# The second product of the MLP by Strassen's scheme, one product of quarters behind the other in four PSUM banks each

## The chip, the core and the metric

The kernel runs on one core of a Trainium2 chip. Five engines work side by side and meet only at semaphores: TensorE (PE in the profile, with its weight loads as PEld), VectorE (DVE), ScalarE (ACT), GpSimd (POOL) and SyncE (SP). Each takes its instructions in order. Operands lie in SBUF, 128 partitions wide; matmul results go to PSUM, which has eight banks of 128 x 512 floats. DMA transfers are issued here by SP. The metric is the device time of one execution in microseconds, as the median of several.

## The reference

One layer of a decoder over 1024 tokens of width 1024: a mixer with two kinds of attention, and an MLP. The change is in the last part of the MLP:

```python
h = rms_norm(x, pre_ffn_g[l])
u = causal_depthwise_conv(h @ w_up[l], conv_w[l], conv_b[l])
gate, val = jnp.split(u, 2, axis=-1)
y = (jax.nn.gelu(gate, approximate=True) * val) @ w_down[l]
x = x + rms_norm(y, post_ffn_g[l])
```

With G for `gelu(gate) * val` (1024 tokens x 2816 features), the last product is Y = G W with W = `w_down` (2816 x 1024). After it come the sum of squares of each row of Y, the gain `post_ffn_g`, and the addition of x.

## The kernel before

Every product is made of float32 operands that are split in two: `hi`, rounded by a copy on ScalarE (line 140), and `lo`, the rest, by a subtraction on VectorE (line 137). A product is then three matmuls, hi x hi, lo x hi and hi x lo, into the same bank. A tile of 128 x 512 thus costs one load of 256 KB, one ACTIVATE and one TENSOR_TENSOR before TensorE can use it. `load_raw` loads such a tile into a pool of five buffers, `slot_w` gives the pair of buffers for hi and lo.

The first product of the MLP (h @ w_up) runs over 22 blocks of 128 features. From block 3 on, `seven` computes a block by seven products of quarters: halves of tokens, of the inner dimension and of gate and value. `weights` makes the sums and splits of the weight quarters one block ahead. `gated` does the convolution and the gate for a block and stores G, transposed, to DRAM as `c_d[f]` (line 1073); this is the last thing done for a block.

The second product, from line 1209 on, runs over halves of the tokens (`half`). For each of 22 feature blocks `down_operands` loads and splits the 512 tokens of `c_d[f]` (tiles `gh`, `gl`) and the two halves of `w_down[f]` (tiles `whi`, `wlo`, from pool `wpool` or `dw`). `product(f, m)` multiplies 128 tokens of it by both halves of the outputs, six matmuls, into two banks that belong to m: four m and two banks each take all eight banks for the whole half. For the last four blocks (`LAST`) the program goes m by m, so that the rows of one m are complete before those of the next. A complete m is finished by lines 1240 to 1249: squares and their sum on ScalarE, the gain on VectorE, the reciprocal root by ten small operations on VectorE (`rsqrt`, lines 153 to 168), then one operation for each half of the outputs that scales and adds x (`x2`), and a store of it.

The operands of feature blocks 0 and 1 are loaded and split during the last block of the first product (line 1201), into the pool `early` and into free slots of `wpool`. Pools open and close like a stack from two sides of SBUF, left and right; a tile of a new pool waits for the tiles that had its place. When the first product ends, its pools close (`mix` with the activations, `uf`, `xw`, `early`, `cv` on the right, `wb` and `mid` on the left), and `gp2` on the left and `dw` on the right take their place.

The order of the instructions on each engine, SP's queue too, is made by a planner: it goes by the order of the program, by when it expects things to be ready, and lets what stands in `tc.high_priority` go ahead. The order of the trace is therefore not always that of the program.

Of the kernel before, what the change touches and what calls it, by code (L numbers as in the profile page):

```python
# [24 lines left out]
P = 128  # L25
S = 1024
D = 1024
# [6 lines left out]
NF = FF // P  # L34
# [7 lines left out]
NEG = -1.0e30  # L42

FULL = 3
LAST = 4
MIX_UNITS = {3: (0,), 4: (1,), 5: (2, 4), 6: (3, 5), 7: (6, 7)}
START_GATES, A_FILLS, B_GATES = 2, ("pggg", "pvgg", "wpgg", "PVg"), 3
SLOTS = 18
# [37 lines left out]
def trunk(ctx: ExitStack, tc: tile.TileContext, a, out):  # L86
    nc = tc.nc
    dma = nc.sync.dma_start

    def open_pool(stack, name, bufs=1, side="left", **kw):  # L90
        if "space" not in kw:
            kw.update(side=side, reuse_waits="tile")
        return stack.enter_context(tc.tile_pool(name=name, bufs=bufs, **kw))
# [17 lines left out]
    def slot_w(pool=None):  # L111

        return [(pool or wpool).tile([P, 512], F32R, tag=t, name=n, bufs=6) for t, n in (("wh", "whi"), ("wl", "wlo"))]

    def load_raw(src, pool=None):
        raw = (pool or raws_in[-1]).tile([P, 512], F32, tag="raw", name="raw", bufs=3 if pool else None)
        dma(raw, src)
        return raw

# [19 lines left out]
    def split(hi, lo, src, eng=None):  # L139
        nc.scalar.activation(hi, src, AF.Copy)  # L140
        sub(eng or nc.vector, lo, src, hi)
# [29 lines left out]
    def halves():  # L171
        return [slice(i * 512, (i + 1) * 512) for i in range(2)]
# [142 lines left out]
    with ExitStack() as st0:  # L315
# [54 lines left out]
        for n, i in enumerate(FIRST_GATES):  # L370
            t = prep.tile([P, S], F32, tag=f"raw{n}", name="gate")
# [16 lines left out]
        for half, sl in enumerate(halves()):  # L388
            row = psum(F32, pt, "pt")
# [314 lines left out]
    for n in range(2):  # L704
        t = mask_2.rearrange("p (k r) -> p r k", r=2)[:, n]
# [237 lines left out]
    def any_psum():  # L943
        return next(psums)()

    with st2:
# [48 lines left out]
        for m in range(8):  # L995
# [5 lines left out]
            pss = []  # L1001
# [128 lines left out]
    def weights(f):  # L1130

        a11, a12, a21, a22 = (load_raw(a["w_up"][2 * f + part][:, sl]) for part in range(2) for sl in halves())
        ws = {}

        def put(name, src):
            ws[name] = slot_w(wb if len(ws) % 2 else None)
            split(*ws[name], src)

        def combined(name, x, y, op):
            t = mid.tile([P, 512], F32, tag="s", name=name, bufs=4)  # L1140
            nc.vector.tensor_tensor(t, x, y, op=op)
# [41 lines left out]
        plus(c12, "p3", c12)  # L1183
        return us

    def down_operands(half, f, pool, bufs, w_pool):

        raw = load_raw(c_d[f][:, halves()[half]], pool if w_pool else None)
        g = [pool.tile([P, 512], F32R, tag=t, name=t, bufs=bufs) for t in ("gh", "gl")]
        split(*g, raw)  # L1190
        us = []
        for sl in halves():
            us.append(slot_w(w_pool))
            split(*us[-1], load_raw(a["w_down"][f][:, sl]))
        return g, us
# [10 lines left out]
    st_x.close()  # L1206


    gp2 = open_pool(ctx, "gp2")
    dw = open_pool(ctx, "dw", side="right")  # L1210
    gpost2 = gp2.tile([P, D], F32, name="gpost2")
    dma(gpost2, a["post_ffn_g"].partition_broadcast(P))
    for half in range(2):
        pss = [psum(F32, pt, "pt") for _ in range(2)] + [any_psum() for _ in range(6)]

        def product(f, m):
            (gh, gl), us = have[f]
            tk = slice(m * P, (m + 1) * P)
            for ps, (wh, wl) in zip(pss[2 * m : 2 * m + 2], us):
                nc.tensor.matmul(ps, gh[:, tk], wh, start=f == 0, stop=False)  # L1220
                nc.tensor.matmul(ps, gl[:, tk], wh, start=False, stop=False)  # L1221
                nc.tensor.matmul(ps, gh[:, tk], wl, start=False, stop=f == NF - 1)  # L1222

        for f in range(NF):
            if half or f not in have:

                with tc.high_priority(offset=60 if half == 0 and f < 4 else 0):
                    have[f] = down_operands(half, f, gp2, 6, dw)
            if f < NF - LAST:
                for m in range(4):  # L1230
                    product(f, m)
        for m in range(4):
            rows = slice((4 * half + m) * P, (4 * half + m + 1) * P)
            x2 = gp2.tile([P, D], F32, tag="x2", name="x2", bufs=3)
            dma(x2, x2_d[rows, :])
            sq, yg = (gp2.tile([P, D], F32, tag=n, name=n, bufs=2) for n in ("sq", "yg"))
            s2 = tiny.tile([P, 2], F32, tag="sm", name="s2")
            for f in range(NF - LAST, NF):
                product(f, m)
            for n, w in enumerate(halves()):  # L1240
                ps = pss[2 * m + n]
                nc.scalar.activation(sq[:, w], ps, AF.Square, accum_out=s2[:, n : n + 1])
                nc.vector.tensor_tensor(yg[:, w], ps, gpost2[:, w], op=ALU.mult)  # L1243
            ss = tiny.tile([P, 1], F32, tag="ss1", name="ss1")
            nc.vector.tensor_tensor(ss, s2[:, 0:1], s2[:, 1:2], op=ALU.add)
            r = rsqrt(ss, D, tiny, "r1")
            for w in halves():
                nc.vector.scalar_tensor_tensor(x2[:, w], yg[:, w], r, x2[:, w], op0=ALU.mult, op1=ALU.add)
                dma(out[rows, w], x2[:, w])


def units(w, rows, cols):
# [51 lines left out]
```

## Time and profile before

| | us |
|---|---|
| median of 3 runs (1812.74 to 1817.44) | 1813.17 |
| the profiled execution's own time | 1812.37 |
| its span, first to last instruction | 1810.6 |
| PE busy in the span | 1756.2 |
| DVE busy in the span | 1251.5 |
| ACT busy in the span | 846.8 |
| second product, first matmul to PE's end | 1546.4 to 1794.0 |
| from there to the end of the span | 16.6 |

The page of the profile gives the busy time of each engine, the same in forty slices of the span, and the chain of work that ended last. A matmul record overlaps the next, so that a busy PE isn't PE at its peak; the pace of matmuls is read from their starts. A row of a group shows its line, engine and operation, the tiles written and read, the count, busy time and mean, and the idle time before it with what ended it. SPq stands for SP's queue of transfers: the time of a record there is that from its issue on, with waits between those that a record merges.

### The profile page before, as it was taken

How to read it: one execution, taken by the hardware profiler on the slowest of the kernel's cores; microseconds unless marked ns; L12 is line 12 of the kernel's file. 1: busy time of each engine (PE TensorE's matmuls, PEld its weight loads, DVE VectorE, ACT ScalarE, POOL GpSimd, SP SyncE). 2: the span in 40 equal slices, each digit the busy share in tenths (PEclk: the TensorE clock that was granted, in tenths of full speed). 3: DMA queues.
4: the chain of work that ended last, by engine and by line, in shares of the span. 5: the costliest groups of instructions: out<-in, count | busy, mean ns of one | idle time of the engine just before them, and what ended most of it. 6: DMA issues, size and time to landing. Idle time of an engine off the chain costs nothing.

```text
span 1810.6 us, 24293 instructions
## 1 busy us (share of the span) xinstructions
PE 1756.2 (97%) x8886; PEld 1488.2 (82%) x8886; DVE 1251.5 (69%) x2509; ACT 846.8 (47%) x1555; POOL 51.0 (3%) x78
## 2 busy tenths in 40 slices
PE   9998999999999999999999999999999999999996
PEld 7987788788888888888777788878888888788785
DVE  4677787775555666555767677999999998434634
ACT  6375455544555644555554332554444343334331
POOL 0000000000000000000001301200000000000000
PEclk9999999999999999999999999999999999999998
DMA  8511121212131334222575421122222222644741
GB/s 268 165 52 37 59 71 59 82 41 65 51 97 53 100 118 146 67 92 94 166 249 195 156 100 64 47 101 98 89 81 76 94 81 88 200 143 142 235 135 64
DMA packets 99831, 195.52 MB, mean 108 GB/s; under 512 B 16304, under 2 KB 23152, under 8 KB 99712
## 3 DMA queue, kind: packets, MB, share of 16 engines
q1 hardware_dynamic: 91616, 182.97, 30.5%
q10 hardware_dynamic: 8096, 11.01, 1.7%
q8 instruction: 69, 1.13, 0.3%
q14 instruction: 50, 0.41, 0.1%
HBM read 150.27 MB, written 43.66 MB: 107 GB/s over the span
## 4 chain that ended last, share of the span: by engine, by line
PE 77%; DVE 9%; DMA 7%; ACT 3%; issue 3%; SPq 0%; POOL 0%; DVEq 0%; ACTq 0%
PE acc L145 14%; PE acc L144 14%; PE acc L146 14%; PE acc L435 3%; PE acc L437 3%; PE acc L436 3%; PE acc L1220 3%; PE acc L1221 3%; PE acc L1222 3%; PE acc L987 2%; PE acc L988 2%; PE acc L986 2%; DMA gl<-gt_d 1%; PE o L481 1%; PE pt L469 1%
## 5 line engine op out<-in xcount | busy, mean ns | idle before, releaser
L140 ACT ACTIVATE whi<-raw 128x512 fp32r<-128x512 f32 (+1 forms) x316 | 195.1, 626 | 342.5 <-PE acc L146 138.0
L137 DVE TENSOR_TENSOR wlo<-raw,whi 128x512 fp32r<-128x512 f32 (+1 forms) x313 | 225.5, 728 | 173.8 <-ACT whi L140 155.5
L144 PE MATMUL acc<-xh,whi 128*128 128x512 f32 x744 | 297.1, 401 | 4.8 <-DVE t L418 2.9
L145 PE MATMUL acc<-xh,wlo 128*128 128x512 f32 x744 | 297.8, 400 | 1.4 <-DVE wlo L137 1.4
L146 PE MATMUL acc<-xl,whi 128*128 128x512 f32 x744 | 295.4, 399 | 0.0
L144 PEld LDWEIGHTS acc<-xh,whi 128*128 128x128 f32 x744 | 140.9, 190 | 33.9 <-DVE t L418 3.3
L145 PEld LDWEIGHTS acc<-xh,wlo 128*128 128x128 f32 x744 | 141.3, 190 | 29.6 <-DVE wlo L137 1.6
L146 PEld LDWEIGHTS acc<-xl,whi 128*128 128x128 f32 x744 | 141.7, 190 | 28.9
L144 PE MATMUL acc<-mh,whi 128*128 128x512 f32 x400 | 156.3, 391 | 1.8 <-ACT whi L140 1.6
L145 PE MATMUL acc<-mh,wlo 128*128 128x512 f32 x400 | 156.3, 391 | 0.2 <-DVE wlo L137 0.2
L146 PE MATMUL acc<-ml,whi 128*128 128x512 f32 x400 | 156.1, 391 | 0.0
L435 PE MATMUL acc<-whi,xh 128*128 128x256 f32 x512 | 147.4, 288 | 0.0
L437 PE MATMUL acc<-wlo,xh 128*128 128x256 f32 x512 | 146.8, 287 | 0.0
L436 PE MATMUL acc<-whi,xl 128*128 128x256 f32 x512 | 146.7, 287 | 0.0
L417 ACT ACTIVATE t<-acc 64x512 f32<-64x512 f32 (+1 forms) x160 | 94.6, 591 | 44.8 <-PE acc L146 42.3
L1172 DVE TENSOR_TENSOR u<-acc,u 128x512 f32<-128x512 f32 x133 | 90.4, 683 | 26.6 <-PE acc L146 26.5
L1220 PE MATMUL acc<-whi,gh 128*128 128x512 f32 x264 | 103.3, 395 | 1.4 <-DVE yg L1243 1.4
L1221 PE MATMUL acc<-whi,gl 128*128 128x512 f32 x264 | 102.7, 389 | 0.0
L1222 PE MATMUL acc<-wlo,gh 128*128 128x512 f32 x264 | 101.6, 389 | 0.0
L436 PEld LDWEIGHTS acc<-whi,xl 128*128 128x128 f32 x512 | 97.7, 191 | 0.8
L435 PEld LDWEIGHTS acc<-whi,xh 128*128 128x128 f32 x512 | 97.8, 191 | 0.6
L437 PEld LDWEIGHTS acc<-wlo,xh 128*128 128x128 f32 x512 | 97.7, 191 | 0.5
(287 smaller groups left out, 3694.9 us busy)
## 6 DMA issues: line engine op xcount, KB each, us to landing
raw<-in_w_in SPq DMA_DIRECT2D x126, 256.0 KB, 2.8
raw<-in_w_up SPq DMA_DIRECT2D x88, 256.0 KB, 2.8
raw<-in_w_down SPq DMA_DIRECT2D x88, 256.0 KB, 3.3
c_d<-c SPq DMA_DIRECT2D x22, 512.0 KB, 2.7
raw<-c_d SPq DMA_DIRECT2D x44, 256.0 KB, 3.5
gl<-gt_d SPq DMA_DIRECT2D x16, 512.0 KB, 5.7
gt_d<-gate ACTq DMA_DIRECT2D x26, 256.0 KB, 2.0
og_d<-osb SPq DMA_DIRECT2D x12, 512.0 KB, 4.5
```

Of the source, the lines that this page charges most:

```text
L137: eng.tensor_tensor(lo, src, hi.bitcast(F32), op=ALU.subtract)
L140: nc.scalar.activation(hi, src, AF.Copy)
L144: nc.tensor.matmul(o, sh, mh, start=first, stop=False)
L145: nc.tensor.matmul(o, sl, mh, start=False, stop=False)
L146: nc.tensor.matmul(o, sh, ml, start=False, stop=last)
L417: nc.scalar.activation(t1[dst], ps[src], AF.Copy)
L435: nc.tensor.matmul(ps, xh[:, k, tk], wh[:, w], start=k == 0, stop=False)
L436: nc.tensor.matmul(ps, xl[:, k, tk], wh[:, w], start=False, stop=False)
L437: nc.tensor.matmul(ps, xh[:, k, tk], wl[:, w], start=False, stop=k == KC - 1)
L1220: nc.tensor.matmul(ps, gh[:, tk], wh, start=f == 0, stop=False)
L1221: nc.tensor.matmul(ps, gl[:, tk], wh, start=False, stop=False)
L1222: nc.tensor.matmul(ps, gh[:, tk], wl, start=False, stop=f == NF - 1)
```

## The change

Y is cut in quarters: tokens in two halves i, features in two halves j of 11 blocks (`NH`), outputs in two halves k. With A for the quarters of G and B for those of W, the seven products are, in the order in which they run:

| | left | right | added to |
|---|---|---|---|
| p1 | A11 | B11 | c11, u |
| p5 | A21 + A22 = S1 | B12 - B11 = T1 | c22, c12 |
| p6 | S1 - A11 = S2 | B22 - T1 = T2 | u |
| p7 | A11 - A21 | B22 - B12 | c21, c22 |
| p3 | A12 - S2 | B22 | c12 |
| p2 | A12 | B21 | c11 |
| p4 | A22 | B21 - T2 | c21 |

with u = p1 + p6, c12 = u + p5 + p3, c21 = u + p7 + p4, c22 = u + p7 + p5, c11 = p1 + p2. A product runs over 11 feature blocks; a step is one block, 4 x 3 matmuls of 128 x 512 into four banks, and the next product takes the other four. The program has 77 steps. `load` issues a step's loads 8 steps ahead (14 from p2 on), `prepare` makes sums and splits some five steps ahead, `product` multiplies, `take` adds a finished product to `ys` in SBUF. The quarters A11, B11 and B12 and the sums are kept in `ax`, `az`, `by`, `bv`, eleven tiles each. Operands have 16 places for a pair hi and lo near the end: six in `wpool`, five in `dw`, five in `more`. The operands of steps 0 to 3 are prepared during the last block of the first product; their quarters are loaded once more for keeping. The finish of rows 0 to 511 stands inside p4, that of the other four row blocks behind it, with the last seven steps of p4 block by block.

```diff
-LAST = 4
+NH = NF // 2
+AHEAD, T1_AT, LAST = 4, 5, 7
...
-    def down_operands(half, f, pool, bufs, w_pool):
...
+    def g_at(i, j, f):
+        return c_d[j * NH + f][:, halves()[i]]
+    def w_at(j, k, f):
+        return a["w_down"][j * NH + f][:, halves()[k]]
+    operands = {}
+    def put(step, *srcs):
+        operands[step] = []
+        for src in srcs:
+            operands[step].append(next(places)())
+            split(*operands[step][-1], src)
+    places = iter([lambda: slot_w(early, 2), slot_w] * 2 + [slot_w] * 4)
     ws = weights(FULL)
-    have = {}
     for f in range(FULL, NF):
         if f + 1 == NF:
-            have.update({i: down_operands(0, i, early, 2, None) for i in range(2)})
+            for i in range(AHEAD):
+                put(i, load_raw(g_at(0, 0, i)), load_raw(w_at(0, 0, i)))
...
+    raws_in.append(open_pool(ctx, "raw_d", side="right", bufs=8))
     dw = open_pool(ctx, "dw", side="right")
...
+    by = row("by", ctx, "right")
+    az = row("az", st_az, "right")
+    ax = row("ax", ctx, "left")
+    yp = open_pool(ctx, "yp")
+    gpost2 = yp.tile([P, D], F32, name="gpost2")
+    ys = [yp.tile([P, D], F32, tag=f"y{m}", name="y") for m in range(8)]
+    bv = row("bv", st_bv, "left")
+    def around():
+        for n in itertools.count():
+            yield (lambda: slot_w(dw, 5)) if n % 11 < 5 else slot_w
...
+    order = ("p1", "p5", "p6", "p7", "p3", "p2", "p4")
+    steps = [(p, f) for p in order for f in range(NH)]
...
+    def load(n):
+        p, f = steps[n]
+        raw = raw_of[n] = []
+        if p == "p1":
+            dma(ax[f], g_at(0, 0, f))
+            dma(by[f], w_at(0, 0, f))
+        if p == "p5":
+            raw += [load_raw(g_at(1, j, f)) for j in range(2)]
+        if p == "p7":
+            raw.append(load_raw(g_at(1, 0, f)))
+        if p in ("p6", "p7", "p3"):
+            raw.append(load_raw(w_at(1, 1, f)))
+        if p == "p3":
+            dma(ax[f], g_at(0, 1, f))
+        if p == "p2":
+            dma(bv[f], w_at(1, 0, f))
+        if p == "p4":
+            raw.append(load_raw(g_at(1, 1, f)))
+        if 0 <= n - T1_AT < NH:
+            dma(bv[n - T1_AT], w_at(0, 1, n - T1_AT))
+    def prepare(n):
+        p, f = steps[n]
+        raw = raw_of.pop(n)
+        if p == "p1" and n >= AHEAD:
+            put(n, ax[f], by[f])
+        if p == "p5":
+            tt(az[f], *raw, op=ALU.add)
+            put(n, az[f], by[f])
+        if p == "p6":
+            tt(az[f], az[f], ax[f])
+            tt(by[f], raw[0], by[f])
+            put(n, az[f], by[f])
+        if p == "p7":
+            tt(ax[f], ax[f], raw[0])
+            tt(bv[f], raw[1], bv[f])
+            put(n, ax[f], bv[f])
...
+        if 0 <= n - T1_AT < NH:
+            tt(by[n - T1_AT], bv[n - T1_AT], by[n - T1_AT])
+    def product(n, m):
+        p, f = steps[n]
+        (gh, gl), (wh, wl) = operands[n]
+        tk = slice(m * P, (m + 1) * P)
+        nc.tensor.matmul(banks[m], gh[:, tk], wh, start=f == 0, stop=False)
+        nc.tensor.matmul(banks[m], gl[:, tk], wh, start=False, stop=False)
+        nc.tensor.matmul(banks[m], gh[:, tk], wl, start=False, stop=f == NH - 1)
+    def take(p, m, ps):
+        (c11, c12), (c21, c22) = ([ys[i * 4 + m][:, sl] for sl in halves()] for i in range(2))
+        if p == "p1":
+            nc.scalar.activation(c11, ps, AF.Copy)
+        if p == "p5":
+            nc.scalar.activation(c22, ps, AF.Copy)
+        if p == "p6":
+            tt(c21, ps, c11, ALU.add)
+            tt(c12, c21, c22, ALU.add)
+        if p == "p7":
+            tt(c21, ps, c21, ALU.add)
+            tt(c22, c21, c22, ALU.add)
...
+    def finish(m):
+        x2 = load_x2(m)
+        nc.vector.tensor_tensor(ys[m], ys[m], gpost2, op=ALU.mult)
+        nc.vector.scalar_tensor_tensor(x2, ys[m], r4[0][:, m : m + 1], x2, op0=ALU.mult, op1=ALU.add)
+        dma(out[m * P : (m + 1) * P, :], x2)
...
+    for n, (p, f) in enumerate(steps):
+        if f == 0:
+            i = n // NH
+            banks = [psum(F32, pt, "pt") for _ in range(0 if i % 2 else 2)] + [any_psum() for _ in range(4 if i % 2 else 2)]
+        if n == 1:
+            dma(gpost2, a["post_ffn_g"].partition_broadcast(P))
+        loaded = reach(loaded, n + (7 if n == 0 else 8 if n < 5 * NH else 14), load)
+        last = p == "p2" and f >= NH - 3
+        if last and f == NH - 3:
+            prepared = reach(prepared, 6 * NH, prepare)
+            st_bv.close()
+            more = open_pool(ctx, "more")
...
+        with tc.high_priority(offset=60 if n == 0 else 0):
+            prepared = reach(prepared, n + (6 if n == 0 else 5) + (2 * (f - NH + 4) if last else 6 if p == "p4" else 0), prepare)
...
+        if p != "p4" or f < NH - LAST:
+            for m in range(4):
+                product(n, m)
+        if p != "p4" and f == NH - 1:
+            for m in range(4):
+                take(p, m, banks[m])
...
+    for m in range(4):
+        rows = slice((4 + m) * P, (5 + m) * P)
+        x2 = load_x2(4 + m)
+        for f in range(NH - LAST, NH):
+            product(6 * NH + f, m)
+        take("p4", m, banks[m])
+        c21 = ys[4 + m][:, :512]
+        sum_squares(c21, sums[m][:, 0:1])
+        nc.vector.tensor_tensor(c21, c21, gpost2[:, :512], op=ALU.mult)
...
+        for sl in halves():
+            nc.vector.scalar_tensor_tensor(x2[:, sl], ys[4 + m][:, sl], r, x2[:, sl], op0=ALU.mult, op1=ALU.add)
+            dma(out[rows, sl], x2[:, sl])
```

More of the change, by code (lines that the diff above doesn't have):

```diff
@@ L109, in trunk, with slot_w, load_raw @@
     raws_in = []
[L111 to L116, printed above, removed]
+    def slot_w(pool=None, bufs=6):
+        return [(pool or wpool).tile([P, 512], F32R, tag=t, name=n, bufs=bufs) for t, n in (("wh", "whi"), ("wl", "wlo"))]
+    def load_raw(src):
+        raw = raws_in[-1].tile([P, 512], F32, tag="raw", name="raw")
         dma(raw, src)
@@ L1206, in trunk @@
     st_x.close()
-    gp2 = open_pool(ctx, "gp2")
+    st_n = ExitStack()
+    raws_in.append(open_pool(ctx, "raw_d", side="right", bufs=8))
     dw = open_pool(ctx, "dw", side="right")
[L1211 to L1229, printed above, removed]
-                for m in range(4):
[L1231 to L1249, printed above, removed]
@@ new lines, in row @@
+    def row(name, stack, side):
+        pool = open_pool(stack, name, side=side)
+        return [pool.tile([P, 512], F32, tag=f"{name}{f}", name=name) for f in range(NH)]
+    st_bv, st_az = ExitStack(), ExitStack()
+    by = row("by", ctx, "right")
[5 more added lines that the diff above has]
+    bv = row("bv", st_bv, "left")
@@ new lines, in prepare @@
+    def prepare(n):
[14 more added lines that the diff above has]
+            put(n, ax[f], bv[f])
+        if p == "p3":
+            tt(az[f], ax[f], az[f])
+            put(n, az[f], raw[0])
+        if p == "p2":
+            put(n, ax[f], bv[f])
+            tt(by[f], bv[f], by[f])
+        if p == "p4":
+            put(n, raw[0], by[f])
+        if 0 <= n - T1_AT < NH:
+            tt(by[n - T1_AT], bv[n - T1_AT], by[n - T1_AT])
@@ new lines, in product @@
+    def product(n, m):
[17 more added lines that the diff above has]
+            tt(c22, c21, c22, ALU.add)
+        if p == "p3":
+            tt(c12, ps, c12, ALU.add)
+        if p == "p2":
+            tt(c11, ps, c11, ALU.add)
+        if p == "p4":
+            tt(c21, ps, c21, ALU.add)
@@ new lines, in sum_squares, with load_x2, norm_first @@
+    def sum_squares(y, to):
+        sq = norms.tile([P, 512], F32, tag="sq", name="sq", bufs=2)
+        nc.scalar.activation(sq, y, AF.Square, accum_out=to)
+    def load_x2(r):
+        x2 = norms.tile([P, D], F32, tag="x2", name="x2", bufs=3)
+        dma(x2, x2_d[r * P : (r + 1) * P, :])
+        return x2
+    r4 = []
+    def norm_first():
+        tt(s4[:, 0], s4[:, 0], s4[:, 1], ALU.add)
+        r4.append(rsqrt(s4[:, 0], D, norms, "r4"))
+    def finish(m):
[3 more added lines that the diff above has]
+        dma(out[m * P : (m + 1) * P, :], x2)
@@ new lines, in trunk, with reach, wider @@
+    sums = [tiny.tile([P, 2], F32, tag="sm", name="sd") for _ in range(4)]
+    prepared = loaded = 0
+    def reach(n, upto, fn):
+        while n < min(upto, len(steps)):
+            fn(n)
+            n += 1
+        return n
+    for n, (p, f) in enumerate(steps):
[10 more added lines that the diff above has]
+            more = open_pool(ctx, "more")
+            old = places
+            def wider():
+                for n in range(16):
+                    yield (lambda: slot_w(more, 5)) if n % 3 == 0 and n < 15 else next(old)
+                yield from old
+            places = wider()
+        with tc.high_priority(offset=60 if n == 0 else 0):
+            prepared = reach(prepared, n + (6 if n == 0 else 5) + (2 * (f - NH + 4) if last else 6 if p == "p4" else 0), prepare)
+        if p == "p2" and f == 0:
+            st_az.close()
+            norms = open_pool(ctx, "norms", side="right")
+            s4 = norms.tile([P, 2, 4], F32, name="s4")
+        if p != "p4" or f < NH - LAST:
[4 more added lines that the diff above has]
+                take(p, m, banks[m])
+        if p == "p2" and 2 <= f < 6:
+            m = f - 2
+            sum_squares(ys[m][:, 512:], s4[:, 1, m : m + 1])
+            sum_squares(ys[4 + m][:, 512:], sums[m][:, 1:2])
+            c22 = ys[4 + m][:, 512:]
+            nc.vector.tensor_tensor(c22, c22, gpost2[:, 512:], op=ALU.mult)
+        if p == "p4" and f < 4:
+            if f == 0:
+                for m in range(4):
+                    sum_squares(ys[m][:, :512], s4[:, 0, m : m + 1])
+                norm_first()
+            finish(f)
```

15 lines of the change are left out of this document (7 added, 8 removed).

## The prediction

> **What bounds the kernel now.** I read the page first: the busy shares, the forty slices and the shares of the chain.
>
> ```profile
> span 1810.6 us, 24293 instructions
> PE 1756.2 (97%) x8886; PEld 1488.2 (82%) x8886; DVE 1251.5 (69%) x2509; ACT 846.8 (47%) x1555; POOL 51.0 (3%) x78
> ...
> DVE  4677787775555666555767677999999998434634
> ...
> PEclk9999999999999999999999999999999999999998
> ...
> PE 77%; DVE 9%; DMA 7%; ACT 3%; issue 3%; SPq 0%; POOL 0%; DVEq 0%; ACTq 0%
> ```
>
> PE is busy 97% of the span at full clock and 77% of the chain is PE. VectorE (DVE) is at nine tenths in the slices of the first product of the MLP and at three to six in the last six slices, where the second product lies. So in the place of the change matmuls set the pace and VectorE has room. Next the busy time by stretch: one inside the first product, which already runs by seven quarter products, then the second product and what follows it.
>
> ```profile
> 1200.00:1500.00 300.00, 300.00 (x1325) 248.39 (x1325) 279.84 (x376) 131.09 (x178) 3.18 (x32) 1.00 0.25 86
> 1546.40:1794.00 247.60, 241.78 (x1057) 198.99 (x1055) 106.18 (x193) 84.96 (x156) 0.00 (x0) 0.99 0.48 156
> 1794.00:1811.00 17.00, 0.00 (x0) 0.00 (x0) 13.05 (x52) 1.82 (x7) 0.00 (x0) 0.61 0.43 155
> ```
>
> Columns: length, then PE, weight loads, DVE, ACT, POOL busy, clock, DMA share, GB/s. The second product takes 247.6 us, DVE 106 of them; 17 us follow in which PE does nothing and DVE 13. The first row matters later: for 300 us PE had no gap although DVE was busy 279.84.
>
> How long is a matmul? A record lasts 0.39 us but the next one starts sooner, so I count starts, in the order-of-time view of PE:
>
> ```profile
> 1546.40 0.39 PE L1220 MATMUL pt<-whi,gh 128*128 128x512 f32 x1
> ...
> 1557.06 0.39 PE L1222 MATMUL acc<-wlo,gh 128*128 128x512 f32 x1
> 1561.86 0.91 PE L1220 MATMUL pt<-whi,gh 128*128 128x512 f32 x2 [4.42 <-ACT gh L140]
> ...
> 1565.84 0.39 PE L1221 MATMUL pt<-whi,gl 128*128 128x512 f32 x1
> ...
> 1793.61 0.39 PE L1222 MATMUL acc<-wlo,gh 128*128 128x512 f32 x1
> ```
>
> The first two rows are the first and 48th matmul of the product: 10.66/47 = **0.2268 us each**. The groups of the stretch from 1545 give the number of matmuls, 3 x (264 + 88) = 1056 (three lines of one count each):
>
> ```profile
> L1220 PE MATMUL acc<-whi,gh 128*128 128x512 f32 x264 | 103.3, 395 | 1.4 <-DVE yg L1243 1.4
> ...
> L137 DVE TENSOR_TENSOR wlo<-raw,whi 128x512 fp32r<-128x512 f32 x84 | 57.0, 691 | 124.5 <-ACT whi L140 107.8 <-PE acc L1221 16.6
> L140 ACT ACTIVATE whi<-raw 128x512 fp32r<-128x512 f32 x84 | 52.2, 630 | 154.6 <-PE acc L1221 133.2 <-PE acc L146 12.0 <-DMA raw<-in_w_down 7.1
> ...
> L1221 PE MATMUL pt<-whi,gl 128*128 128x512 f32 x88 | 34.5, 392 | 0.0
> ...
> L1243 DVE TENSOR_TENSOR yg<-acc,gpost 128x512 f32<-128x512 f32 x12 | 7.8, 680 | 0.0
> ...
> L161 DVE TENSOR_SCALAR r1w<-r1y,r1v 128x1 f32<-128x1 f32 x24 | 5.9, 265 | 0.0
> L162 DVE TENSOR_SCALAR r1y<-r1w,r1y 128x1 f32<-128x1 f32 x24 | 4.5, 204 | 0.1
> ```
>
> 1056 x 0.2268 = 239.5 us. From first to last start are 247.2, so 7.7 us are stalls: 4.6 in the gap before 1561.86, 1.7 because the ten matmuls from there take 3.98 us in place of 2.27, and 1.4 where the second half begins. Window rows of 10 us show the last two, with the clock at 0.83 in the first and PE at 8.60 of 10 in the second:
>
> ```profile
> 1560.00:1570.00 10.00, 8.14 (x29) 6.53 (x30) 2.72 (x5) 3.06 (x6) 0.00 (x0) 0.83 1.00 354
> 1680.00:1690.00 10.00, 8.60 (x38) 6.77 (x37) 9.52 (x20) 2.90 (x6) 0.00 (x0) 1.00 0.90 303
> ```
>
> **The change, term by term.** The sum is made in the profiled execution: span 1810.6, its own time 1812.37, so 1.8 us lie around the span; the median of the runs, 1813.17, is 0.8 above that.
>
> *Matmuls.* Seven products of 11 steps of 4 blocks of 3 are 924. 924 x 0.2268 = **209.6 us**; 132 go, 29.9 us. A step of 12 is 2.72 us, a product 29.9. As PE waits for nothing in most of the stage, this comes off the end in full unless something else becomes late.
>
> *What VectorE gets.* Back to back an operation of 512 columns costs less than its 0.69 us record. Five splits in a row, and ScalarE's five beside them:
>
> ```profile
> 1547.27 3.10 DVE L137 TENSOR_TENSOR wlo<-raw,whi 128x512 fp32r<-128x512 f32 x5
> ```
> ```profile
> 1546.60 2.72 ACT L140 ACTIVATE whi<-raw 128x512 fp32r<-128x512 f32 x5 [12.02 <-PE acc L146]
> ```
>
> (3.10 - 0.69)/4 = **0.60 us** on DVE; ACT 0.54, two per step, 1.1 of 2.72 us, no bound. The new sums (88, two inputs in SBUF) aren't in the second product before; the nearest rows are these splits, also two inputs and one output, and I take 0.60 with 0.69 as the upper end. DVE by product, splits + sums + sums with a bank: p1 14+6 = 20 operations, 12 us (four steps are split earlier); p5 38, 23 us; p6 44, 26 us; p7 44 and p6's eight, 52, 31 us; p3 41, 25 us; p2 41, 25 us (with four multiplications); p4 26, 16 us, and for the four early rows eight operations of 1024 columns at twice 0.60 and a root of some 2.5, together 28. Only p7 exceeds its 29.9 us of PE, by 1.3, and operands are prepared four steps (10.9 us) ahead. Cost: nothing while that lead stands. The sums with p1 and p5 go to ACT, the others read a bank that is needed again two products later, 29.9 us, so no bank is waited for.
>
> The Trainium skill, "VectorE: DVE Perf Modes", section "The DRAIN you can't avoid", has the next operation wait until the pipe is empty, unless it isn't held. By full records of 0.69 us p6 and p7 would need 66.2 of PE's 59.9 us, 6.3 more than they have; the trace's 0.60 speaks against that. It is in a rival below.
>
> *The start.* Here the trace of before has its largest gap, and its cause is in the queue of SP and on ACT:
>
> ```profile
> 1547.99 7.19 SPq L117 DMA_DIRECT2D raw<-in_w_down  x6
> 1557.37 0.33 SPq L1073 DMA_DIRECT2D c_d<-c  x1
> 1557.79 0.38 SPq L117 DMA_DIRECT2D raw<-c_d  x1
> 1558.23 0.77 SPq L1212 DMA_DIRECT2D gpost<-in_post_ffn_g  x1
> ```
> ```profile
> 1561.18 0.63 ACT L140 ACTIVATE gh<-raw 128x512 fp32r<-128x512 f32 x1 [5.87 <-DMA raw<-c_d]
> ```
>
> The third step's activation load was issued only behind the store of the last feature block, whose data VectorE had finished just before; it came 3.4 us later, and PE had run out at 1557.3. Afterwards PE has the same cover: four steps of 12 in place of two of 24, 10.9 us. The fifth step needs loads nine and ten (the first eight bring the quarters of steps 0 to 3 once more, to be kept). Ten of 0.262 MB at the 354 GB/s of the window above are 7.4 us, the first landing takes 2.6 beyond its transfer (3.4 - 0.7), both splits 1.9. Their places: `ax` lies first on the left, where weights of the first product were, `by` on the right over its activations, free when its last matmul ends, 1546.6. Issued then, the operands are ready at 1558.5, 1.2 us late. Issued behind the store, at 1557.8, they are ready at 1569.7: 12.4 us late, and 1.7 of slow clock. Both ends stand, 0 and 14; I take **2 us**, as these tiles don't need what the store waits for.
>
> *The feed.* Loads: 132 of 256 KB as before, and those eight. Up to the last step of p5 there are 55, and the gain row of 0.5 MB: 15 MB in 59.9 us, 250 GB/s; later less. The nearest row for a long stretch is
>
> ```profile
> 1550.00:1600.00 50.00, 45.58 (x194) 37.21 (x193) 22.72 (x31) 17.42 (x28) 0.00 (x0) 0.97 0.66 217
> ```
>
> 217 GB/s at a share of 0.66, so not full, and 354 at 1.00. Between nothing (15 MB at 354 are 42 us) and 9 us (at 217, 69 us) I take nothing, since 217 was what was asked for. The Trainium skill, "SBUF — State Buffer", section "The DMA setup-cost knee", gives 224 GB/s for transfers of 256 KB; an estimate from it is 67 us, 7 more than PE needs. The 354 of this trace, with several transfers queued, is above that figure.
>
> *Other stalls.* Six product changes and the packed VectorE: between 0 (the 300 us row) and 8.4 (1.4 each, as at the old half change, which had no free bank). I take **3 us**, nearer the first as four banks are free each time.
>
> *The tail.* Before, all four row blocks end together:
>
> ```profile
> 1785.63 1.37 DVE L137 TENSOR_TENSOR wlo<-raw,whi 128x512 fp32r<-128x512 f32 x2 [12.23 <-PE acc L1221]
> ...
> 1805.02 0.27 DVE L161 TENSOR_SCALAR r1w<-r1y,r1v 128x1 f32<-128x1 f32 x1
> 1805.32 0.21 DVE L162 TENSOR_SCALAR r1y<-r1w,r1y 128x1 f32<-128x1 f32 x1
> 1805.57 0.15 DVE L168 TENSOR_SCALAR r1y<-r1y 128x1 f32<-128x1 f32 x1
> 1806.12 1.41 DVE L1248 SCALAR_TENSOR_TENSOR x<-yg,r1y,x 128x512 f32<-128x512 f32 x2 [0.39 <-DVE r1y L168]
> ```
> ```profile
> 1791.09 0.60 ACT L1242 ACTIVATE sq<-pt 128x512 f32<-128x512 f32 x1 [4.81 <-PE pt L1222]
> 1791.58 0.19 ACT L1242 ACTIVATION_READ_ACCUMULATOR sq<-pt 128x1 f32 x1
> ```
>
> The last weights were split at 1785.6, 12 us after the split before them, when slots came free, so the code's row-by-row order could not be kept; after PE's end at 1794.0 VectorE worked through four rows and the span ended 16.6 us later. Afterwards seven steps need 14 slots and there are 16 (6 + 5 + 5). A row block then has 21 matmuls, 4.8 us, and VectorE needs per row: sum from the bank 0.68, gain 0.6, root about 2.2, two last operations 1.4: 4.9 us, with gaps filled by the next row. So one row is left behind the last matmul: 0.68 for the sum, 0.7 for ACT's square and its readout, 2.5 for the ten dependent small operations (records 0.15 to 0.27, with the gaps of the rows above), 1.4, and 3.1 from the end of the last operation (1807.5) to the end of the span for the store: **8.5 us** in place of 16.6. Rows 0 to 3, done inside p4, lie beside 29.9 us of PE.
>
> *Sum.* 1546.4 + 209.6 + 2 + 3 + 0.2 (end of the last matmul) = 1761.2; + 8.5 = 1769.7; + 1.8 = **1771.5 us**. That is 41.7 below the median: 29.9 from matmuls, 8.1 from the tail, about 2.7 from stalls, 0.8 from the execution chosen. Alone it may lie between 1765 (no stall at all is 1766.5) and 1777.
>
> **The rivals.**
> 1. *The first loads stand behind the store.* SP's queue is in order and the first load of before did just that. For it: those rows; against: other places in memory. 12 us more: 1783.6.
> 2. *The rows end together again.* The planner, not the program, orders PE, and if a split of the last three steps waits for a slot, the tail stays 16.6: 1779.6.
> 3. *VectorE or the feed falls behind, mildly.* 0.69 us per operation without lead, 6 us, or loads at 217 GB/s, 9 us: 1778 to 1787. This is where the rules of the two pages would lead.
> 4. *Slower: a chain between VectorE and ScalarE in p5 to p2.* Each summed operand goes sum (DVE 0.69), upper part (ACT 0.63), lower part (DVE 0.69), and VectorE takes its queue in order. If each link were waited out, a step of p6 and p7 costs 4.0 us against 2.72, 33 us in 22 steps with p6's sums; p5, p3, p2 3.3 us, 20 us in 33. In all 53: 1825. It decides from 47 us, which is 197 us of VectorE for these 216 operations, 0.91 us each. Against: the 300 us row, where sums and splits of the same kind, prepared a block ahead, held PE at 100%.
> 5. *The change doesn't do what it says.* The number of matmuls is fixed by the loops; only their waits can take the gain back, which is 1 to 4.
>
> **Chances.** Forecast 0.58, rival 1 0.14, rival 2 0.09, rival 3 0.10, rival 4 0.06, and 0.03 for a mixture that eats 36 to 47 us and ends within 0.3% of before. 0.3% is 5.4 us, about what a measurement can tell. So faster 0.91, same 0.03, slower 0.06. The range reaches from 1764, under the sum without stalls, to 1790, over rivals 1, 2 and 3: 0.91 less what mixtures of them add above it, some 0.85.
>
> **What would show it.** 924 matmuls 0.227 us apart and 210 to 218 us from first to last; SP issuing `ax` and `by` before the last store to `c_d`; no PE gap over 3 us at the fifth step; PE at full clock through p6 and p7 with DVE near nine tenths; one row of work, 8 to 9 us, behind the last matmul. A PE gap of 10 us at the start says rival 1; a tail of 16 us rival 2; PE waiting for `wlo` or `gl` from DVE in p6 to p3 rivals 3 and 4. The prediction is wrong if PE loses over 20 us in waits, or if the new early splits delay the first product so that the second starts later than 1546.

## The result, and the profile after

| | before | after |
|---|---|---|
| median of 4 runs each, us | 1815.18 (1812.74 to 1817.44) | 1770.0 (1767.12 to 1773.4) |
| the profiled execution's own time | 1812.37 | 1767.12 |
| its span | 1810.6 | 1765.3 |
| second product, first to last matmul start | 247.21 | 209.84 |
| from PE's end to the end of the span | 16.6 | 11.2 |

The ratio is 0.9752, with a 95% interval of 0.9726 to 0.9778: 45 us less. 1771.5 had been forecast. The page of the changed kernel, for comparison with the lines of before:

```profile
span 1765.3 us, 24106 instructions
PE 1721.8 (98%) x8754; PEld 1459.4 (83%) x8754; DVE 1329.9 (75%) x2612; ACT 865.3 (49%) x1585; POOL 51.6 (3%) x78
...
DVE  4667786776556667565665867799999999789978
...
PE 78%; DVE 9%; DMA 7%; issue 3%; ACT 3%; SPq 1%; POOL 0%; DVEq 0%; ACTq 0%
```

TensorE has 8886 - 8754 = 132 matmuls less, as counted. VectorE, which stood at three to six tenths in the last six slices, now stands at seven to nine, and still TensorE's share went up. The order-of-time view of PE gives the stage itself (start, duration, engine, line, operation, count, idle time before it and what ended it):

```profile
1543.88 0.39 PE L1300 MATMUL pt<-whi 128*128 128x512 f32 x1
...
1554.54 0.39 PE L1302 MATMUL acc<-wlo,whi 128*128 128x512 f32 x1
1555.25 0.73 PE L1300 MATMUL pt<-whi 128*128 128x512 f32 x2 [0.33 <-ACT whi L143]
...
1753.72 0.39 PE L1302 MATMUL acc<-wlo,whi 128*128 128x512 f32 x1
```

From 1543.88 to 1753.72 are 209.84 us; 923 steps of 0.2268 are 209.3. The whole second product waits 0.5 us, all of it at 1555.25, the first matmul of the fifth step. Nothing is lost at the six product changes or in the products with many sums.

What stood beside it shows in the busy time by stretch (length, then PE, weight loads, DVE, ACT, POOL, clock, DMA share, GB/s):

```profile
1550.00:1560.00 10.00, 9.67 (x43) 7.70 (x42) 7.64 (x11) 5.50 (x9) 0.00 (x0) 1.00 1.03 386
...
1570.00:1580.00 10.00, 10.00 (x46) 8.29 (x45) 9.60 (x17) 6.93 (x13) 0.00 (x0) 1.00 1.03 379
1590.00:1620.00 30.00, 30.00 (x134) 24.82 (x134) 30.00 (x51) 16.21 (x30) 0.00 (x0) 1.00 0.63 204
...
1650.00:1680.00 30.00, 30.00 (x134) 24.86 (x133) 30.00 (x51) 13.85 (x23) 0.00 (x0) 1.00 0.42 132
1680.00:1710.00 30.00, 30.00 (x134) 24.82 (x134) 20.00 (x32) 17.51 (x38) 0.00 (x0) 1.00 0.23 79
```

Two resources are full, and PE loses almost nothing by it. At the start the DMA engines move 386 and 379 GB/s at a share of 1.03, and the 0.5 us fall into this stretch. From 1590 to 1680 VectorE is busy 30.00 of 30 us, 51 operations in each 30, and PE is at 30.00 too.

SP's queue and ScalarE at the start:

```profile
1543.89 0.33 SPq L1253 DMA_DIRECT2D by<-in_w_down  x1
1544.27 0.42 SPq L1252 DMA_DIRECT2D ax<-c_d  x1
...
1554.50 0.33 SPq L1253 DMA_DIRECT2D by<-in_w_down  x1
1555.07 0.33 SPq L1076 DMA_DIRECT2D c_d<-c  x1
```
```profile
1553.07 0.63 ACT L143 ACTIVATE whi<-ax 128x512 fp32r<-128x512 f32 x1 [2.15 <-DMA ax<-c_d]
1554.57 0.63 ACT L143 ACTIVATE whi<-by 128x512 fp32r<-128x512 f32 x1 [0.86 <-DMA by<-in_w_down]
```

The loads of `ax` and `by` go from 1543.89 on, in turn (one of `ax` had gone before), and the last store to `c_d` follows only at 1555.07. The last upper part that the fifth step needs was made from 1554.57 on, after a wait of 0.86 us for its load, just as PE ran out.

The tail, VectorE in order of time; L1246 takes a finished row block out of its bank, L1408 is the gain, L1413 the two last operations:

```profile
1741.68 0.69 DVE L1246 TENSOR_TENSOR y<-pt,y 128x512 f32<-128x512 f32 x1 [0.19 <-PE pt L1302]
...
1744.62 0.69 DVE L1246 TENSOR_TENSOR y<-pt,y 128x512 f32<-128x512 f32 x1 [0.27 <-PE pt L1302]
...
1750.73 0.68 DVE L1246 TENSOR_TENSOR y<-acc,y 128x512 f32<-128x512 f32 x1
...
1753.38 1.42 DVE L1413 SCALAR_TENSOR_TENSOR x<-y,r1y,x 128x512 f32<-128x512 f32 x2
...
1754.89 0.68 DVE L1246 TENSOR_TENSOR y<-acc,y 128x512 f32<-128x512 f32 x1
...
1756.42 0.69 DVE L1408 TENSOR_TENSOR y<-y,gpost 128x512 f32<-128x512 f32 x1 [0.17 <-ACT sq L1326]
...
1757.90 1.40 DVE L1413 SCALAR_TENSOR_TENSOR x<-y,r1y,x 128x512 f32<-128x512 f32 x2
...
1760.78 1.42 DVE L1413 SCALAR_TENSOR_TENSOR x<-y,r1y,x 128x512 f32<-128x512 f32 x2
```

The rows no longer end together: they are taken at 1741.7, 1744.6, 1750.7 and 1754.9. PE had ended at 1754.11, so the last sum comes 0.8 us late, because VectorE was still at the two last operations of the second row (1753.38). From there to the end of the last operation at 1762.20 are 7.3 us, and the last operations of the third row (1757.90) lie among them. 3.1 more to the end of the span make 11.2.

So the 45.3 us between the two spans are 29.9 of matmuls, 7.5 of waits in the product, 5.4 of the tail, and 2.5 because this execution began the product earlier. The last of these can't be put down to the change: the kernels below that leave the first product as it is here began the second anywhere from 1542.1 to 1552.2, in one profiled execution each, and why is open.

### The profile page after: what moved, and what is told of

It is laid out like the page before. It is cut to its first block, busy times and chain, and to the rows that moved or that the text cites. A ratio compares the mean times of both kernels' runs of the same rounds, so it can differ in the third digit from the quotient of the medians.

```text
span 1765.3 us, 24106 instructions
## 1 busy us (share of the span) xinstructions
PE 1721.8 (98%) x8754; PEld 1459.4 (83%) x8754; DVE 1329.9 (75%) x2612; ACT 865.3 (49%) x1585; POOL 51.6 (3%) x78
## 4 chain that ended last, share of the span: by engine, by line
PE 78%; DVE 9%; DMA 7%; issue 3%; ACT 3%; SPq 1%; POOL 0%; DVEq 0%; ACTq 0%
PE acc L148 15%; PE acc L147 15%; PE acc L149 15%; PE acc L438 3%; PE acc L440 3%; PE acc L439 3%; PE acc L1301 3%; PE acc L1300 3%; PE acc L1302 3%; PE acc L990 2%; PE acc L991 2%; PE acc L989 2%; PE o L484 2%; PE pt L472 1%; DMA og<-og_d 1%
## 5 line engine op out<-in xcount | busy, mean ns | idle before, releaser
L143 ACT ACTIVATE whi<-raw 128x512 fp32r<-128x512 f32 (+1 forms) x258 | 158.8, 624 | 208.5 <-PE acc L149 125.2
L140 DVE TENSOR_TENSOR wlo<-raw,whi 128x512 fp32r<-128x512 f32 (+1 forms) x255 | 185.0, 732 | 47.3 <-ACT whi L143 45.8
L143 ACT ACTIVATE whi<-s 128x512 fp32r<-128x512 f32 x76 | 47.2, 628 | 105.2 <-PE acc L149 96.0
L147 PEld LDWEIGHTS acc<-mh,whi 128*128 128x128 f32 x400 | 75.5, 189 | 18.2 <-ACT whi L143 2.1
L148 PEld LDWEIGHTS acc<-mh,wlo 128*128 128x128 f32 x400 | 75.5, 189 | 16.2 <-DVE wlo L140 0.5
```

Source lines behind the costliest of these rows:

```text
L140: eng.tensor_tensor(lo, src, hi.bitcast(F32), op=ALU.subtract)
L147: nc.tensor.matmul(o, sh, mh, start=first, stop=False)
L148: nc.tensor.matmul(o, sl, mh, start=False, stop=False)
```

## The experiments

Two questions were open. How much of the 45 us is Strassen's scheme, and how much came only from the new order of loads and the new places? And how near are the rivals: the start behind the store, rows that end together, VectorE? The medians come from several measurements, in which the kernel before took between 1812.72 and 1815.18 us; a difference of two or three us between two kernels can't be told from them, and smaller ones are read from the traces, of one execution each.

**Before, with more places (b_slots).** The pool `dw` gives eight pairs for weights in place of six, so that the last steps of a half find their places.

```diff
-    def slot_w(pool=None):
+    def slot_w(pool=None, bufs=6):
...
-            us.append(slot_w(w_pool))
+            us.append(slot_w(w_pool, 8 if w_pool else 6))
```

> The kernel before, with eight places instead of six for split weights in dw, so that all eight pairs of the last four blocks fit. Theory (part of the gain is the tail, and the tail came from missing places): PE ends as before, near 1794, and the time from there to the end of the span goes from 16.6 us to between 8.5 and 11; the whole is 5 to 8 us shorter than before. Rival (the tail belongs to the finish of the rows, whatever the places): 16 us stay and the whole is within 2 us of before.

Measured: 1805.66 us beside 1812.86, ratio 0.9957 (0.994 to 0.9974), 7.2 less and so within the 5 to 8. The tail fell from 16.6 to 8.6 us, so the old tail was indeed a matter of places and not of Strassen's scheme. But PE's end didn't stay near 1794. In the profiled execution, the slowest of the four, it came at 1798.4 and the span is only 3.6 us shorter: the product began 1.8 later, and the gap at the start grew from 4.6 to 8.0:

```profile
1567.13 1.22 PE L1220 MATMUL pt<-whi,gh 128*128 128x512 f32 x2 [7.86 <-ACT gh L140]
```

SP now issued eight loads of weights ahead of the store instead of six; the activation load behind it went out at 1560.6 and its split began only at 1566.45.

**The same, with the operands in another pool (b_slots_start).** The activations' pairs move from `gp2` to `dw`, so that their first loads needn't wait for what lay on the left.

```diff
-                    have[f] = down_operands(half, f, gp2, 6, dw)
+                    have[f] = down_operands(half, f, dw, 6, dw)
```

> The same, and the activations of the second product are loaded and split in pool dw on the right in place of gp2 on the left. Theory (the gap at the start is a load that stands behind the last store because of its place in memory): the third block's load is issued before that store, the gap of 4.8 us and the slow matmuls behind it go, 5 to 7 us beside the 5 to 8 of the tail: 10 to 15 us less than before, and what then separates it from the changed kernel is the 132 matmuls, 30 us. Rival (all of the 45 us come from the matmuls): no change from before, and 45 us to the changed kernel.

Measured: 1797.09 us, ratio 0.9921 (0.9899 to 0.9944), 15.8 less than before and a little over the 10 to 15. The product takes 239.14 us from first to last matmul; 1055 steps of 0.2268 are 239.3. No wait is left:

```profile
1545.76 0.39 PE L1220 MATMUL pt<-whi,gh 128*128 128x512 f32 x1
...
1784.90 0.39 PE L1222 MATMUL acc<-wlo,gh 128*128 128x512 f32 x1
```
```profile
1545.78 0.33 SPq L117 DMA_DIRECT2D raw<-c_d  x1
...
1559.93 0.33 SPq L1073 DMA_DIRECT2D c_d<-c  x1
```
```profile
1785.42 1.31 DVE L1243 TENSOR_TENSOR yg<-acc,gpost 128x512 f32<-128x512 f32 x2 [0.37 <-ACT sq L1242]
...
1789.43 1.41 DVE L1248 SCALAR_TENSOR_TENSOR x<-yg,r1y,x 128x512 f32<-128x512 f32 x2 [0.40 <-DVE r1y L168]
```

The first load of activations goes out at 1545.78, the store at 1559.93. VectorE is done with each row before it starts on the next, and with the last it needs 5.4 us (1785.42 to 1790.84); the tail is 8.6. Against this kernel, the changed one has 29.3 us less between first and last matmul and a tail 2.6 us longer; its median is 27.1 us lower, from another measurement. Some 16 us of the gain (1812.86 - 1797.09) could be had with the old scheme.

**The place of ax (a_ax_late).** Of the changed kernel, the eleven tiles `ax` are laid behind `yp` on the left in place of ahead of it, so that they fall on other memory of the first product.

```diff
-    ax = row("ax", ctx, "left")
     yp = open_pool(ctx, "yp")
...
     ys = [yp.tile([P, D], F32, tag=f"y{m}", name="y") for m in range(8)]
+    ax = row("ax", ctx, "left")
```

> The changed kernel with the places of ax and of yp swapped on the left, so that the tiles of A11 lie where the last block's convolution still works. Theory (place in memory decides whether the first loads go ahead of the last store): the loads of ax fall behind that store and behind the loads queued in between, some thirty of 0.74 us; the fifth step is 14 to 22 us late, PE idles there, and the whole is 14 to 24 us longer than the changed kernel. Rival (the four steps prepared early cover it): under 4 us.

Measured: 1794.78 us, ratio 0.9898 (0.9882 to 0.9915), 24.8 above the changed kernel; the spans of the two profiled executions differ by 22.9.

```profile
1557.87 0.33 SPq L1076 DMA_DIRECT2D c_d<-c  x1
...
1567.87 6.98 SPq L1252 DMA_DIRECT2D ax<-c_d  x11
```
```profile
1577.09 1.22 PE L1300 MATMUL pt<-whi 128*128 128x512 f32 x2 [21.65 <-ACT whi L143]
```

The loads of `ax` fall behind the store, and also behind thirteen others that the planner then puts first: they go out at 1567.87, and PE stands 21.65 us at the fifth step. Rival 1 was real; which tiles lie where decides over more than half of the change.

**Without the five late places (a_no_more).** The pool `more` and `wider` are left out; eleven places remain for the 14 operands of the last seven steps.

```diff
-            more = open_pool(ctx, "more")
-            old = places
...
-            places = wider()
```

> The changed kernel without the pool more, so that p4 has 11 places for the 14 pairs of its last seven steps. Theory (the places make the short tail): the last splits wait until places come free, the four row blocks end together again and the tail goes from 11.2 us to between 14 and 18: 3 to 7 us longer. Rival (the planner's order, not the places): within 1.5 us of the changed kernel.

Measured: 1781.04 us, ratio 0.9823 (0.9809 to 0.9838), 11.0 above the changed kernel, where 3 to 7 had been expected. The tail grew to 21.3 us:

```profile
1757.32 1.29 DVE L1246 TENSOR_TENSOR y<-pt,y 128x512 f32<-128x512 f32 x2 [3.72 <-PE pt L1302]
1758.52 1.28 DVE L1246 TENSOR_TENSOR y<-acc,y 128x512 f32<-128x512 f32 x2
...
1774.99 1.41 DVE L1404 SCALAR_TENSOR_TENSOR x<-y,r1y,x 128x512 f32<-128x512 f32 x2 [4.18 <-DMA x<-x_d]
```

All four rows are taken between 1757.3 and 1759.8, as in the kernel before, and the last waits another 4.18 us for its load of x, which has only three buffers. Rival 2 was real too, and dearer than its 16.6.

**VectorE loaded further (a_dve1, a_dve3).** One or three more subtractions of two tiles into a tile that nothing reads, in each step of p6 and p7: 22 or 66 operations. For three, the diff has 3 in place of 1.

```diff
+    scr = yp.tile([P, 512], F32, name="scr")
...
             tt(by[f], raw[0], by[f])
+            for _ in range(1):
+                tt(scr, az[f], ax[f])
...
             tt(bv[f], raw[1], bv[f])
+            for _ in range(1):
+                tt(scr, ax[f], by[f])
```

> The changed kernel with one more subtraction of 128x512 on VectorE in each step of p6 and p7, whose result nobody reads: 22 operations. Theory (0.60 us each back to back, operands four steps ahead): 70.9 us of VectorE stand against 59.9 of PE in p6 and p7, the lead of 10.9 us covers the difference, PE waits 0 to 5 us and the whole is 0 to 5 us longer than the changed kernel. Rival (0.69 us each, as their records last): 81.4 against 59.9, PE waits 9 to 15 us.

> The same with three more in each of those steps, 66 operations. Theory (0.60 us): 97.2 us against 59.9, less the lead of 10.9: PE waits 22 to 32 us, the whole is as much longer. Rival (0.69 us): 111.7 against 59.9, 38 to 46 us. If p7 and p3 hid more (VectorE has slack in p3 and p2), under 15 us.

Measured: 1773.87 us, ratio 0.9777 (0.9754 to 0.9799), with one, and 1805.6, ratio 0.9963 (0.9947 to 0.998), with three. From first to last matmul the product takes 214.56 and 245.81 us, 4.7 and 36.0 more than without. 4.7 lies in the theory's range. 36.0 doesn't: it is above the theory's 22 to 32 and below the rival's 38 to 46. With one there are two gaps over a microsecond:

```profile
1586.47 1.20 PE L1306 MATMUL acc<-whi,wlo 128*128 128x512 f32 x4 [1.23 <-DVE wlo L140]
```
```profile
1678.56 0.73 PE L1306 MATMUL pt<-whi,wlo 128*128 128x512 f32 x2 [1.51 <-DVE wlo L140]
```

The first is in p5 and the second in p3, not in p6 and p7: VectorE works ahead, and the planner puts the sums for p6 among those for p5. With three, p5 loses 4 us, p7 some 11 and p3 some 22.

22 operations of 0.60 are 13.2 us of VectorE, of which 4.7 reach the end: the lead and the room before and behind the full stretch took 8.5. The next 44 cost 31.3 us, 0.71 each, 0.11 more than the 0.60. With three, the matmuls also ran more slowly for a time, at a lower clock:

```profile
1670.00:1700.00 30.00, 22.17 (x73) 14.66 (x73) 29.69 (x49) 6.91 (x12) 0.00 (x0) 0.83 0.35 106
1700.00:1730.00 30.00, 22.02 (x82) 14.10 (x81) 29.79 (x50) 11.16 (x21) 0.00 (x0) 1.00 0.42 131
```
```profile
1683.62 1.22 PE L1306 MATMUL pt<-whi,wlo 128*128 128x512 f32 x2 [1.75 <-DVE wlo L140]
...
1685.50 1.05 PE L1307 MATMUL pt<-wlo,whi 128*128 128x512 f32 x2
1686.35 1.05 PE L1307 MATMUL acc<-wlo,whi 128*128 128x512 f32 x2
1689.02 1.22 PE L1305 MATMUL pt<-whi 128*128 128x512 f32 x2 [1.62 <-ACT whi L143]
```

Between these waits the matmuls start 0.43 apart (1685.50 to 1686.35 for two), where 0.227 is the pace otherwise. But that isn't shown to be the reason for the 0.11. VectorE did 49 operations in the 30 us at a clock of 0.83 and 50 in the 30 us at 1.00, and stood idle for 0.3 us or less in each; from 1574 to 1733 it did 260 in 159 us, 0.61 each. So VectorE itself set the pace, and most of the 0.11 stays open; the order in which the planner mixes the added operations with those that TensorE waits for is a candidate that wasn't tried. What is shown is that VectorE is a true limit here, 8.5 us away, and that behind it an operation costs at least its full time.

**Less for VectorE ahead of the tail (a_tail).** The gain of c12 is multiplied in p2, so that `finish` has half as much to do in p4, and x gets six buffers.

```diff
-        x2 = norms.tile([P, D], F32, tag="x2", name="x2", bufs=3)
+        x2 = norms.tile([P, D], F32, tag="x2", name="x2", bufs=6)
...
-        nc.vector.tensor_tensor(ys[m], ys[m], gpost2, op=ALU.mult)
+        nc.vector.tensor_tensor(ys[m][:, :512], ys[m][:, :512], gpost2[:, :512], op=ALU.mult)
...
-            nc.vector.tensor_tensor(c22, c22, gpost2[:, 512:], op=ALU.mult)
+            for c in (ys[4 + m][:, 512:], ys[m][:, 512:]):
+                nc.vector.tensor_tensor(c, c, gpost2[:, 512:], op=ALU.mult)
```

> The changed kernel with the gain of c12 multiplied in p2 as that of c22 is, so that each of the four early rows needs 512 columns less in p4, and six buffers instead of three for x2. Theory (the tail is 11.2 us and not 8.5 because VectorE still works on rows that should be done when PE ends): the tail goes to between 8.5 and 9.5 us, the whole is 1.5 to 2.7 us shorter than the changed kernel. Rival (the dependent small operations of the last row set the tail): within 0.7 us of 11.2.

Measured: 1768.34 us, ratio 0.9745 (0.9725 to 0.9764), which is no difference from the changed kernel, and a tail of 11.8 us. This theory of the tail fell:

```profile
1739.54 0.68 DVE L140 TENSOR_TENSOR wlo<-by,whi 128x512 fp32r<-128x512 f32 x1
1745.45 1.29 DVE L1246 TENSOR_TENSOR y<-pt,y 128x512 f32<-128x512 f32 x2 [5.23 <-PE pt L1302]
```

VectorE had done everything by 1740.2 and stood 5.23 us until the first row block came, and with it the second: the planner had mixed the last matmuls of m = 0 and m = 1. Rows 0 to 3 weren't what the tail waited for. 11.8 is within the rival's 0.7 of 11.2, but with the two rows mixed this execution doesn't single out the small operations.

**Longer row blocks (a_last9).** The last nine steps go row block by row block instead of seven, with nine places in `more`. A row then has 27 matmuls, 6.1 us.

```diff
-AHEAD, T1_AT, LAST = 4, 5, 7
+AHEAD, T1_AT, LAST = 4, 5, 9
...
-                for n in range(16):
-                    yield (lambda: slot_w(more, 5)) if n % 3 == 0 and n < 15 else next(old)
+                for n in range(20):
+                    yield (lambda: slot_w(more, 9)) if n % 2 == 0 and n < 18 else next(old)
```

> The changed kernel with the last nine steps of p4 row block by row block in place of seven, and nine places in pool more in place of five. Theory: the tail of 11.2 us is made of four rows of some 5 us of VectorE, one behind the other from the end of the first row block (1741.7, 12.4 before the last matmul). With 27 matmuls a row block takes 6.1 us of TensorE, more than VectorE's 5, so each row is done before the next sum and only the last is left: a tail of 8.5 to 9.3 us, a time of 1765 to 1766 (within the measurement of the changed kernel), and VectorE idle between the rows waiting for PE. Rival: it is the last row's chain itself, or the stores, that needs 11 us behind the last matmul: the tail stays at 10.5 to 11.5. Second rival: steps 68 to 76 need 18 of 20 places and their operands come late: PE waits for whi or wlo in p4, over 2 us, and the time is that of the changed kernel or above.

Measured: 1771.65 us, ratio 0.9761 (0.9742 to 0.9781): no difference that can be told. Its second product has no gap of 0.25 us (209.22 us from first to last). The tail is 10.4 us, above the theory's 8.5 to 9.3 and 0.1 under what the rival had given. VectorE in order of time:

```profile
1761.80 0.69 DVE L1246 TENSOR_TENSOR y<-acc,y 128x512 f32<-128x512 f32 x1 [1.09 <-PE acc L1302]
...
1763.34 0.69 DVE L1408 TENSOR_TENSOR y<-y,gpost 128x512 f32<-128x512 f32 x1 [0.17 <-ACT sq L1326]
...
1764.24 1.42 DVE L1413 SCALAR_TENSOR_TENSOR x<-y,r1y,x 128x512 f32<-128x512 f32 x2
...
1767.62 1.42 DVE L1413 SCALAR_TENSOR_TENSOR x<-y,r1y,x 128x512 f32<-128x512 f32 x2
```

Now VectorE waits for PE ahead of the last row's sum (1.09 us), so this sum is no longer late. Yet the last row takes 7.2 us, from 1761.80 to 1769.04, because the row before isn't finished by then: the rest of its root stands behind that sum in the queue. The gain (L1408) waits for ScalarE, since it overwrites the tile that ScalarE is squaring; and the two last operations of the row before (L1413 at 1764.24) come only behind that gain. The theory had the step wrong that each row would be done before the next sum.

**The gain in a tile of its own (a_last9_out).** As above, and:

```diff
-        nc.vector.tensor_tensor(c21, c21, gpost2[:, :512], op=ALU.mult)
+        yg = norms.tile([P, 512], F32, tag="yg", name="yg", bufs=2)
+        nc.vector.tensor_tensor(yg, c21, gpost2[:, :512], op=ALU.mult)
...
-        for sl in halves():
-            nc.vector.scalar_tensor_tensor(x2[:, sl], ys[4 + m][:, sl], r, x2[:, sl], op0=ALU.mult, op1=ALU.add)
+        for sl, y in zip(halves(), (yg, ys[4 + m][:, 512:])):
+            nc.vector.scalar_tensor_tensor(x2[:, sl], y, r, x2[:, sl], op0=ALU.mult, op1=ALU.add)
```

> The kernel with nine last steps per row block, and the gain of a row block's quarter c21 written to a tile of its own in place of over c21. Theory: in the run before, the last row needed 7.2 us of VectorE's queue from its sum to its last operation, and 0.9 of them waited for ScalarE, because the gain overwrites what the square still reads, while the row before's two last operations (1.3 us) came only behind the gain. With a tile of its own the gain needn't wait and those two fall beside the square: 6.0 to 6.4 us from sum to end, a tail of 9.1 to 9.6 in place of 10.4, no operation of L1409 waiting for ACT. The time stays within the measurement of the changed kernel (1768 to 1772). Rival: the chain goes through the square and the sum of squares, not through the gain, and the tail stays at 10.2 to 10.6.

```profile
1758.02 0.69 DVE L1246 TENSOR_TENSOR y<-acc,y 128x512 f32<-128x512 f32 x1 [0.93 <-PE acc L1302]
1758.62 0.74 DVE L1414 SCALAR_TENSOR_TENSOR x<-yg,r1y,x 128x512 f32<-128x512 f32 x1
...
1759.95 0.69 DVE L1409 TENSOR_TENSOR yg<-y,gpost 128x512 f32<-128x512 f32 x1
...
1763.64 0.75 DVE L1414 SCALAR_TENSOR_TENSOR x<-y,r1y,x 128x512 f32<-128x512 f32 x1
```

Measured: 1769.55 us, ratio 0.9753 (0.9734 to 0.9773), again the same as the changed kernel, and a tail of 9.5 us. The row before is finished beside ScalarE's square, the gain no longer waits, and from the sum to the end are 6.4 us (1758.02 to 1764.39). Both figures lie in the theory's ranges, though the planner's order also changed beside the edit: here the root of the row before was done ahead of the last sum. Its 1.7 us, out of 1770, can't be seen in the medians, and no version here can be called faster than the changed kernel.

## Why the prediction was right

The prediction's sum was 1769.7 for the span, and 1765.3 was measured; the median lies 2.9 above the profiled execution, and so the final figure came 1.5 from the mark. That closeness is partly luck. In the span, the product began 2.5 earlier than was taken, the wait at its start was 1.5 and the other stalls 3 shorter, and the tail was 2.7 longer, 4.4 in all with the roundings; the median then happened to lie 2.9 the other way. The mechanism, 132 matmuls that come off the end in full, was right. Term by term:

- *Matmuls, 209.6.* Right. 132 went, the pace stayed 0.2268, and they came off the end in full.
- *Start, 2 us.* 0.5. "These tiles don't need what the store waits for" held: the loads went out ahead of the store. a_ax_late shows what the step hung on: laid elsewhere, the same tiles cost 21.8 us at that place, where rival 1 had put 12 to 14. The rival counted only the store; it left out the loads that the planner moves ahead in the meantime.
- *Feed, nothing.* Right. What was asked for in the first 30 us was more than the 250 GB/s of the working, and up to 386 were given. The bound of 9 us from 217 GB/s wasn't one. The Trainium skill, "SBUF — State Buffer", section "The DMA setup-cost knee", has 224 GB/s for a transfer of 256 KB; 386 and 379 GB/s, with such loads queued behind each other, are above that, so it is no bound for a queue.
- *Other stalls, 3 us.* 0. No wait stands at a product change, and VectorE's lead covered p7. That the four free banks are the reason for the first wasn't tried.
- *VectorE, nothing.* Right, and its price of 0.60 too: from 1589 to 1679 it did 150 operations in 90.00 us. It was full rather than "near nine tenths". So neither half of rival 3 happened. The measured room is 8.5 us. The Trainium skill, "VectorE: DVE Perf Modes", section "The DRAIN you can't avoid", also has an operation that isn't held start earlier; 0.60 from start to start with records of 0.68 agrees with that, and not with a full record each.
- *Tail, 8.5.* 11.2; the term that was mis-sized. The working had one row of 0.68 + 0.7 + 2.5 + 1.4 left behind the last matmul and let "gaps filled by the next row" cost nothing. In a queue that is taken in order, what fills the gaps of one row delays another: the last sum came 0.8 us late, the gain of the last row (0.6) and the two last operations of the row before (1.3) stood within its chain. a_last9 took away the first and a_last9_out most of the last, and 9.5 were left.
- *Rival 2.* Didn't happen, and a_no_more shows that the five places are the reason.
- *Rival 4.* The limit was put at 0.91 us for each of 216 operations, 197 us of VectorE. a_dve3 adds 40 us and is still 7 under before; at 0.71 us for each more, some ten operations further both would be equal. That is an estimate: (130 + 46)/216 = 0.81 us each. So the limit is nearer than it was put. But what a_dve3 shows is a VectorE that is full; that every link between VectorE and ScalarE would be waited out, as the rival had it, no run shows.
- *The first product, start at 1546.4.* 1543.9 here. It was taken as fixed, and among the changed kernels, one profiled execution of each, it lay up to 10 us apart; the prediction's range had no term for that, and its sign "later than 1546" couldn't tell a delay by the early splits from this spread.

What the prediction didn't say is that some 16 of the 45 us belong to places and order, and not to the scheme. It counted 8.1 for the tail and 2.7 for stalls as parts of the change, and two small edits to the kernel before yield such terms as well.

## What to carry to other kernels

Before a new scheme is priced, repair the waits of the old one on paper, and split the gain in two: what goes with the work and what goes with the places. When tiles are laid into memory that another stage leaves, look which of them the first late operand needs, and what its load stands behind in the queue; the order of two lines was worth 25 us here. An engine may run full beside another without costing anything, as VectorE did here for 90 us, but its room should be measured, by adding work until it shows.

## What the runs showed of the hardware

VectorE at 30.00 of 30 us for 90 us held TensorE back by nothing, though it was making the operands that TensorE read some steps later. The DMA engines gave 372 to 386 GB/s over 30 us (1550 to 1580 in the changed kernel) at a share of 1.03 to 1.05, mostly with 256 KB transfers.

The clock of TensorE fell behind some waits and not behind others. In a_dve3 it was 0.83 from 1670 to 1700, with waits of 2.13, 1.75 and 1.62 us in the middle of it, and matmuls started 0.43 us apart; from 1700 to 1730, with waits of up to 1.76, it was 1.00. In a_dve1 it was 1.00 from 1590 to 1680 with a single wait of 1.51, and in b_slots the matmuls behind a single wait of 7.86 started 0.43 apart for some five us. No rule comes out of these runs. The Trainium skill, "TensorE: Matmul & The Clock Gate", section "Wait — 56ns, not 53.3ns?", gives 426.7 ns from start to start for 512 columns at the lower of two clocks, which the 0.85 us for two in the rows of a_dve3 agree with.
